# Scalar bias on the copies out of PSUM, one addition per projection, a third bank for q, and lag products with their sides exchanged

## The chip, the cores and the metric

The kernel runs on one core of one Trainium2 chip. The metric is the device time of one execution in microseconds (us): the median of several runs, and beside it one execution that the hardware profiler recorded. The engines are named as the profile names them: PE (TensorE matmul), PEld (TensorE weight load), DVE (VectorE), ACT (ScalarE), POOL (GpSimd) and SP (SyncE, which issues most DMAs here).

## The reference, cut to what matters

One layer over a sequence of 2048 rows of 1024 channels:

```python
hn = rmsnorm(h, g)
u, g_ssm, q, k, v, g_attn = jnp.split(hn @ w_in, SPLITS, axis=-1)    # 512 columns each
y_ssm = s5_branch(u, ...) * silu(g_ssm)         # 32 groups of 16 channels, 64 complex states each
y_att = stick_breaking_branch(q, k, v, ...) * silu(g_attn)           # 8 heads of 64
h = h + concat([y_ssm, y_att]) @ w_out
h = h + sigmoid(rmsnorm(h, g2) @ w_ple_gate) * (p @ w_ple_proj)

# stick breaking, per head and block of 128 queries
z = q @ k.T * scale                             # q and k RMS-normed per head
log_stay = where(s < t, log_sigmoid(-z), 0)
later = reverse_cumsum(log_stay) - log_stay
weights = where(s < t, exp(log_sigmoid(z) + later), 0)
out = weights @ v
```

## The kernel before, in words

**Stages.** The stream runs in five stages. First the norms, the u projection and the tables of the state-space model (0 to some 135 us). Then eight batches of the state-space model, four groups each, between which the gate projection of that branch is worked off (`gate_unit`) and the first four attention projections are made (to some 331 us). Then 40 attention steps `t` (to some 1130 us), four passes of two heads (`hp`) that start eight steps apart (SKEW = 8), so that two passes run at a time. Then the output projection and the gated layer embedding (to the end).

**A batch of the state-space model.** `ssm_pack` (L307) builds for four groups `bn` (128 states x 4 groups x 16 lags x 16 channels) and `mc`. It transposes `bn` into `mb` through PSUM (L340, L341), and then makes the lag products: for each of 2 halves `s` and 4 groups `k` one fp32 matmul with the 128 columns of `bn` as the stationary side and the 16 columns of the group's C matrix as the moving side (L346), all into one bank, copied to `lags` by ACT (L349), corrected by DVE and sent to `lag_d` by SP (L355). `ssm_batch` (L370) reads it back later as a Toeplitz matrix.

**A projection.** `attn_proj` (L706) makes q, k, the gate and v of one block of 128 rows for two heads: 512 columns. From the fifth block on it runs with the contraction cut into two halves of 64 rows that run side by side in the array, each into its own bank (L733, 48 records of 64x512). ACT copies the first bank to `part` (L740, or L736 with the row scale for the first two blocks), and DVE adds the second bank to it in two instructions: 384 columns into `qn` (q, k, gate) and 128 columns into `vr` (v); both show as L65, the line of the helper `vt`. The banks go to the next projection when both have read them. Attention needs v minus the row before it. So SP copies rows 0 to 126 of `vr` one partition down into `v` (L743), and the last row of the previous block into row 0 (L747, one row of 512 bytes), and POOL subtracts (L749). POOL also makes the power of the norm (L501) and the causal fill (L812).

**A block of attention.** `attn_block` (L788) goes through the keys in chunks of up to 512, from the last. For each head z = q k in three float32r products (L805), a sigmoid of -z by ACT (L809), the causal fill by POOL on the diagonal chunk (L812), a running product by DVE (L814, reading z's bank once more), then PE transposes (L520, `ps_wt`), and ACT writes 1 minus the transposed product to `ws` (L828): function Identity, scale -1, and for the bias a column of ones in SBUF, `e.one`. PE multiplies `ws` by v (L836), two heads side by side in two halves of the array's columns.

**Banks.** PSUM has eight banks. `BANKS` (L44) deals out six of them: three to z, two to the projection and one to the output of a block up to step 31, and from step 32 on two, two and one, the rest to the GLU.

**The order of the work.** The order on every engine is written out before the program is built: `plan` (L1293) collects what each instruction depends on, `duration` (L1260) gives each a modelled length, `list_schedule` (L1419) lists them forward and backward for six turns, and the best by its own clock is kept. It charges 0.2 for each change between three kinds of PE work: full array, halves by rows, halves by columns (L1419, `change=0.2`). The hardware queues are in order, so an instruction that waits holds all that stand behind it on its engine or queue.

## Time and profile before

| what | value |
|---|---|
| median of 3 runs | 1534.51 us (1533.57 to 1535.1) |
| the profiled execution | 1535.16 us |
| its span, first to last instruction | 1533.4 us |
| PE, PEld busy | 1467.1, 1247.9 us |
| DVE, ACT, POOL busy | 1011.0, 835.4, 494.7 us |
| mean granted TensorE clock | 0.987 |

The profiled execution is 1.8 us longer than its span and 0.65 us longer than the median of the runs. In the rows, a group is a line, an engine, an operation, out<-in and a shape with its count; then its busy time and the mean duration of one in ns; then the idle time of the engine just before these instructions and which instruction ended it. A wait row gives who waited for whom, the total, the count and the longest. A timeline row gives start, length, engine, line, operation and count; neighbours of one kind are merged. PE records overlap: a record's length holds its passage through the array, and the distance from start to start is what it costs.

### The profile page before, as it was taken

How to read it: one execution, taken by the hardware profiler on the slowest of the kernel's cores; microseconds unless marked ns; L12 is line 12 of the kernel's file. 1: busy time of each engine (PE TensorE's matmuls, PEld its weight loads, DVE VectorE, ACT ScalarE, POOL GpSimd, SP SyncE). 2: the span in 40 equal slices, each digit the busy share in tenths (PEclk: the TensorE clock that was granted, in tenths of full speed). 3: DMA queues.
4: the chain of work that ended last, by engine and by line, in shares of the span. 5: the costliest groups of instructions: out<-in, count | busy, mean ns of one | idle time of the engine just before them, and what ended most of it. 6: DMA issues, size and time to landing. Idle time of an engine off the chain costs nothing. (4 is left out here: it accounts for less than half of the span.)

```text
span 1533.4 us, 33754 instructions
## 1 busy us (share of the span) xinstructions
PE 1467.1 (96%) x13116; PEld 1247.9 (81%) x13116; DVE 1011.0 (66%) x1861; ACT 835.4 (54%) x1756; POOL 494.7 (32%) x530
## 2 busy tenths in 40 slices
PE   6999999989999999999999998999999999999998
PEld 5899989978888888888888877777776888777776
DVE  8933868856666786668766777456668556754543
ACT  5644545546555776567665667555654435633333
POOL 3251344412221211212112244431145654434433
PEclk8999999989999999999999999999999999999999
DMA  8877645555432442334333467754457645522211
GB/s 291 281 258 214 222 139 177 180 164 185 144 123 96 141 132 95 125 111 133 124 114 106 145 222 228 239 159 98 105 181 227 206 161 185 184 63 96 89 63 62
DMA packets 179072, 240.33 MB, mean 157 GB/s; under 512 B 65648, under 2 KB 120928, under 8 KB 167520
## 3 DMA queue, kind: packets, MB, share of 16 engines
q1 hardware_dynamic: 176528, 229.58, 46.3%
q0 software_dynamic: 2384, 8.59, 2.1%
q8 instruction: 104, 1.70, 0.5%
q14 instruction: 56, 0.46, 0.1%
HBM read 169.03 MB, written 64.90 MB: 153 GB/s over the span
## 5 line engine op out<-in xcount | busy, mean ns | idle before, releaser
L814 DVE TENSOR_TENSOR_SCAN px<-px,ps_z 128x512 f32<-128x512 f32 (+3 forms) x320 | 341.3, 1086 | 97.0 <-ACT px L809 62.8
L733 PE MATMUL ps_q<-w_w,xt 64*128 64x512 f32 x2880 | 397.5, 401 | 5.7 <-DVE vr L65 5.3
L733 PEld LDWEIGHTS ps_q<-w_w,xt 64*128 64x128 f32 x2880 | 288.7, 187 | 46.3 <-PE ps_z L805 5.5
L828 ACT ACTIVATE ws<-ps_wt,one 128x512 f32<-128x512 f32 (+3 forms) x320 | 189.0, 626 | 86.5 <-PE ps_wt L520 85.2
L809 ACT ACTIVATE px<-ps_z 128x512 f32<-128x512 f32 (+3 forms) x320 | 159.3, 534 | 57.7 <-PE ps_z L805 56.7
L805 PE MATMUL ps_z<-k,q 64*128 64x512 f32 (+3 forms) x960 | 140.3, 379 | 8.2 <-DVE px L814 6.8
L836 PE MATMUL ps_o<-ws,v 128*64 128x128 f32 x2176 | 137.2, 278 | 2.9 <-ACT ws L828 2.9
L836 PEld LDWEIGHTS ps_o<-ws,v 128*64 128x64 f32 x2176 | 118.6, 138 | 19.6 <-issue 12.6
L520 PEld LDWEIGHTS ps_wt<-ident,px 64*128 64x128 f32 x2176 | 98.2, 139 | 32.8 <-ACT ws L828 15.7
L501 POOL TENSOR_TENSOR rs_qk<-rs_qk,mhalf 128x4 f32<-128x4 f32 x64 | 67.5, 1055 | 144.9 <-DVE rs_qk L72 144.6
L520 PE MATMUL ps_wt<-ident,px 64*128 64x64 f32 x2176 | 105.1, 225 | 9.3 <-ACT ws L828 8.4
L805 PEld LDWEIGHTS ps_z<-k,q 64*128 64x128 f32 x960 | 91.3, 187 | 25.3 <-DVE px L814 9.6
L812 POOL TENSOR_SCALAR_AFFINE_SELECT px<-px 128x128 f32<-128x128 f32 x128 | 40.5, 324 | 211.8 <-ACT px L809 196.7
L749 POOL TENSOR_TENSOR v<-vr,v 128x128 f32<-128x128 f32 x64 | 31.2, 488 | 195.6 <-DMA v<-vr 195.6
L535 PE MATMUL ps_u<-xt,w_w 128*128 128x256 f32 x256 | 75.2, 296 | 8.1 <-ACT w_w L485 6.9
L1008 POOL TENSOR_TENSOR sg<-sg,h 128x512 f32<-128x512 f32 x32 | 44.8, 1411 | 112.7 <-DVE sg L65 112.7
L65 DVE TENSOR_TENSOR yr<-sx,yr 128x512 fp32r<-128x512 f32 x64 | 56.3, 900 | 34.1 <-ACT yr L507 33.1
L537 PE MATMUL ps_u<-xt,w_w 128*128 128x256 f32 x256 | 74.6, 298 | 2.5 <-DVE w_w L76 2.5
L65 DVE TENSOR_TENSOR qn<-ps_q,part 128x384 f32<-128x384 f32 x54 | 29.5, 547 | 71.3 <-ACT part L740 68.7
L536 PE MATMUL ps_u<-xt,w_w 128*128 128x256 f32 x256 | 75.1, 295 | 0.5 <-DVE xt L65 0.5
L507 ACT ACTIVATE yr<-sx 128x512 fp32r<-128x512 f32 x64 | 39.3, 628 | 54.5 <-PE ps_h L703 19.7
L535 PEld LDWEIGHTS ps_u<-xt,w_w 128*128 128x128 f32 x256 | 51.8, 202 | 8.7 <-ACT w_w L485 7.1
(416 smaller groups left out, 3490.6 us busy)
## 6 DMA issues: line engine op xcount, KB each, us to landing
xt<-hn SPq DMA_DIRECT2D x60, 1024.0 KB
hn<-xt SPq DMA_DIRECT2D x16, 1024.0 KB
h<-h SPq DMA_DIRECT2D x64, 256.0 KB
wst<-in_w_in_dram SPq DMA_DIRECT2D x48, 256.0 KB
xg<-hn SPq DMA_DIRECT2D x12, 1024.0 KB
out_dram<-sg SPq DMA_DIRECT2D x32, 256.0 KB
x<-in_x_dram SPq DMA_DIRECT2D x14, 512.0 KB
h<-in_x_dram SPq DMA_DIRECT2D x28, 256.0 KB
```

Source lines behind the costliest of these rows:

```text
L65: nc.vector.tensor_tensor(out, a, b, op=op)
L501: nc.gpsimd.tensor_tensor(r, r, e.mhalf[:, :n], op=ALU.pow)
L520: e.nc.tensor.transpose(ps[h][:, 64 * k:64 * k + 64], v[r], e.ident[r, r])
L535: mm(out, wh, xh, start=first, stop=False)
L536: mm(out, wh, xl, start=False, stop=False)
L537: mm(out, wl, xh, start=False, stop=last)
L733: nc.tensor.matmul(o, xt[r, a, c], A.w[c][r, b], start=c + s == 0, stop=c == NC8 - 1 and s == 2)
L805: nc.tensor.matmul(z[:, :n], q[half[h], a], A.k[ch][half[h], b, :n], start=s == 0, stop=s == 2)
L809: nc.scalar.activation(px[:, :n], z[:, :n], AF.Sigmoid, scale=-(HD ** -0.5))
L814: nc.vector.tensor_tensor_scan(rv, rv, z[:, :n][:, ::-1], initial=1.0 if carry[h] is None else carry[h], op0=ALU.mult, op1=ALU.bypass)
L828: nc.scalar.activation(dst, ps, AF.Identity, bias=e.one, scale=-1.0)
L836: nc.tensor.matmul(po[half[h], :P], A.v[sb][:, h], w[:, h, b], start=sb == i, stop=sb == 0)
```

## The change

It does four things.

1. ACT's copy of the transposed products (L828) becomes function Copy with the number 1.0 as bias, in place of Identity with the column `e.one`; the column and its memset go.
2. `qn` becomes 512 columns wide and holds v too. One DVE addition (or one scaled addition for the first two blocks) writes all of it; for blocks 0 to 3 one ACT copy. `vr` is now a view of `qn`. The last row of a block is sent on to row 0 of the next block's v by the same projection, so the v tile of block i+1 is taken one projection earlier; for block 4, whose place doesn't exist yet, the row rests in a small tile `vl` and is copied on by one more DMA. The row DMA still follows the 127-row DMA in SP's queue.
3. In the attention steps 0 to 5 z has two banks and the projection three; from step 6 on all is as before. The names of the two banks become one name that goes round two or three tags.
4. The lag products: C and its turned form now lie in one tile, so that 32 consecutive columns can be taken from every group on. They are the stationary side, `bn` (256 columns for both halves) is the moving side, and the four groups write four strips of 32 partitions of one bank. ACT copies this to `lt` (a tile shared with `part`), PE transposes it in two pieces into another bank, and ACT copies every first 16 of 32 columns to `lags`. The modelled length of such a matmul is cut to a quarter in `duration`.

```diff
--- before.py
+++ after.py
@@ -41,7 +41,7 @@
 XB, XTB, GTB, QSB, PXB, WSB, SWB, ROTB, STA, STB, STC, ALT, ALT0, ALT1, SSM_STEPS, SSM_DEPTH, PREP0, PXX, WSX, XTX, XT0 = 4, 2, 5, 5, 8, 5, 2, 2, 3, 2, 3, "o", 0, 30, 10, 2, 0, 0, 0, 0, 13
 WE = 6
 AHEAD = 4
-BANKS = (("z0", "z1", "tr"), ("acc","ssm"), ("o",)), (("z0", "z1"), ("acc","tr"), ("o",))
+BANKS = (("z0", "z1", "tr"), ("acc", "ssm"), ("o",)), (("z0", "z1"), ("acc", "tr"), ("o",)), (("z0", "z1"), ("acc", "ssm", "tr"), ("o",))
 WSV = lambda ch: 0
 KV_SLOT = {(0, 0): 0, (0, 1): 1, (0, 2): 2, (1, 0): 3, (0, 3): 4, (1, 1): 5, (1, 2): 6, (2, 0): 7,
            (1, 3): 0, (2, 1): 1, (2, 2): 2, (3, 0): 4, (3, 1): 3, (2, 3): 5, (3, 2): 0, (3, 3): 1}
@@ -199,8 +199,8 @@
 
     bst = sm.tile([P, G, GH], F32, tag="bst", name="bst")
     bsw = sm.tile([P, G, GH], F32, tag="bsw", name="bsw")
-    R.cts = kt("cts", [G, GH])
-    R.ct2 = kt("ct2", [G, GH])
+    R.ct = kt("cts", [2, G, GH])
+    R.cts, R.ct2 = R.ct[:, 0], R.ct[:, 1]
     for d, name in ((bst, "b"), (bsw, "b_turned"), (R.cts, "c"), (R.ct2, "c_turned")):
         dma(d, e.small(name).rearrange("p (g h) -> p g h", g=G))
     vs(nc, R.cts, R.cts, sgn, ALU.mult)
@@ -340,13 +340,19 @@
             nc.tensor.transpose(ps[:, k * P:(k + 1) * P], bnf[:, 4 * q + k], e.ident)
         nc.scalar.activation(mbf[:, 4 * q:4 * q + 4].rearrange("p g m -> p (g m)"), ps, AF.Copy)
     ps = e.bank("ps_pack", "w0", "w1")
+    flat = R.ct.rearrange("p k g h -> p (k g h)")
+    with e.abreast():
+        for k in range(GB):
+            o = (b * GB + k) * GH
+            nc.tensor.matmul(ps[2 * GH * k:2 * GH * (k + 1), :HS * P], flat[:, o:o + 2 * GH], bnf[:, HS * k:HS * (k + 1)].rearrange("p s m -> p (s m)"), start=True, stop=True)
+    lt = e.spare.tile([P, 512], F32, tag="part", name="lt", bufs=1)[:, :HS * P]
+    nc.scalar.activation(lt, ps[:, :HS * P], AF.Copy)
+    ps = e.bank("ps_pack", "w0", "w1")
     for s in range(HS):
-        for k in range(GB):
-            o = (s * GB + k) * GH
-            nc.tensor.matmul(ps[:, o:o + GH], bnf[:, HS * k + s], R.cts[:, b * GB + k, :], start=True, stop=True)
+        nc.tensor.transpose(ps[:, s * P:(s + 1) * P], lt[:, s * P:(s + 1) * P], e.ident)
     lags = sm.tile([P, HS + 1, GB, GH], F32, tag="lags", name="lags", bufs=2)
     nc.vector.memset(lags[:, HS], 0.0)
-    nc.scalar.activation(lags[:, :HS], ps[:, :HS * GB * GH].rearrange("p (s g h) -> p s g h", s=HS, h=GH), AF.Copy)
+    nc.scalar.activation(lags[:, :HS], ps[:, :HS * P].rearrange("p (s g v h) -> p s g v h", s=HS, v=2, h=GH)[:, :, :, 0], AF.Copy)
     q3 = slice(96, P)
     sh3 = [P - 96, GB, GH]
     dg = sm.tile([P, GB, GH], F32, tag="dg", name="dg")
@@ -709,22 +715,28 @@
     if xt is None:
         xt = e.buf("xt", [P, 2, NC8, P], XTB, XTX, F32R)
         e.xdma(xt.rearrange("p s c t -> p (s c t)").bitcast(F32), e.hn_d[i])
-    both = pool.tile([P, 3 * HPP, HD], F32, tag="qn", name="qn", bufs=2)
-    vb = A.v[i] = e.kv_tile(A.hp, i, "v", [P, HPP, HD])
-    vr = pool.tile([P, P], F32, tag=f"vr{A.hp % 2}", name="vr", bufs=2)
-    flat, vf, vb = both.rearrange("p h d -> p (h d)"), vr, vb.rearrange("p h d -> p (h d)")
+    both = pool.tile([P, 4 * HPP, HD], F32, tag="qn", name="qn", bufs=2)
+    if i == 0:
+        A.v[i] = e.kv_tile(A.hp, i, "v", [P, HPP, HD])
+        nc.gpsimd.memset(A.v[i][:1], 0.0)
+    if i + 1 < NT and i + 1 not in A.v:
+        A.v[i + 1] = e.kv_tile(A.hp, i + 1, "v", [P, HPP, HD]) if xt is None or i + 1 < AHEAD else pool.tile([P, HPP, HD], F32, tag="vl", name="vl", bufs=1)
+    if A.v[i].tensor.name.startswith("vl"):
+        row = A.v[i]
+        A.v[i] = e.kv_tile(A.hp, i, "v", [P, HPP, HD])
+        nc.sync.dma_start(A.v[i][:1], row[:1])
+    flat, vb = both.rearrange("p h d -> p (h d)"), A.v[i].rearrange("p h d -> p (h d)")
+    vr = flat[:, 384:]
     if len(e.q_banks) == 1:
         pq = e.bank("ps_qk", *e.q_banks)
         for c in range(NC8):
             mm3x(e, pq, (xt[:, 0, c], xt[:, 1, c]), (A.w[c][:, 0], A.w[c][:, 1]), c == 0, c == NC8 - 1)
         if i < 2:
-            nc.scalar.activation(flat, pq[:, :384], AF.Copy, scale=e.rs[i])
-            vs(nc, vf, pq[:, 384:], e.rs[i], ALU.mult)
+            nc.scalar.activation(flat, pq, AF.Copy, scale=e.rs[i])
         else:
-            nc.scalar.activation(flat, pq[:, :384], AF.Copy)
-            nc.vector.tensor_copy(vf, pq[:, 384:])
+            nc.scalar.activation(flat, pq, AF.Copy)
     else:
-        pq = [e.bank(f"ps_q{h}", tag) for h, tag in enumerate(e.q_banks)]
+        pq = [e.bank("ps_q", *e.q_banks) for h in range(2)]
         for c in range(NC8):
             with e.abreast():
                 for s, (a, b) in enumerate(((0, 0), (0, 1), (1, 0))):
@@ -734,20 +746,15 @@
         part = pool.tile([P, 512], F32, tag="part", name="part", bufs=1)
         if i < 2:
             nc.scalar.activation(part, pq[0], AF.Copy, scale=e.rs[i])
-            stt(nc, flat, pq[1][:, :384], e.rs[i], part[:, :384], ALU.mult, ALU.add)
-            stt(nc, vf, pq[1][:, 384:], e.rs[i], part[:, 384:], ALU.mult, ALU.add)
+            stt(nc, flat, pq[1], e.rs[i], part, ALU.mult, ALU.add)
         else:
             nc.scalar.activation(part, pq[0], AF.Copy)
-            vt(nc, flat, pq[1][:, :384], part[:, :384], ALU.add)
-            vt(nc, vf, pq[1][:, 384:], part[:, 384:], ALU.add)
+            vt(nc, flat, pq[1], part, ALU.add)
     nc.sync.dma_start(vb[1:], vr[:P - 1])
-    if A.last is None:
-        nc.gpsimd.memset(vb[:1], 0.0)
-    else:
-        nc.sync.dma_start(vb[:1], A.last[P - 1:])
-    A.last = vr
+    if i + 1 < NT:
+        nc.sync.dma_start(A.v[i + 1][:1].rearrange("p h d -> p (h d)"), vr[P - 1:])
     nc.gpsimd.tensor_tensor(vb, vr, vb, op=ALU.subtract)
-    raw, gate = both[:, :2 * HPP], flat[:, 256:]
+    raw, gate = both[:, :2 * HPP], flat[:, 256:384]
     gn = pool.tile([P, P], F32, tag="gn", name="gn", bufs=1)
     nc.scalar.activation(gn, gate, AF.Sigmoid)
     vt(nc, gn, gate, gn, ALU.mult)
@@ -825,7 +832,7 @@
             if h and WSV(ch):
                 vs(nc, dst, ps, -1.0, ALU.mult, 1.0, ALU.add)
             else:
-                nc.scalar.activation(dst, ps, AF.Identity, bias=e.one, scale=-1.0)
+                nc.scalar.activation(dst, ps, AF.Copy, bias=1.0, scale=-1.0)
         held.append((ch, nb, w))
         if len(held) == HOLD or ch == 0:
             with e.abreast():
@@ -842,7 +849,7 @@
 
 def attn_pass(e, hp):
     A = Env()
-    A.hp, A.k, A.v, A.q, A.w, A.last = hp, [], {}, {}, [], None
+    A.hp, A.k, A.v, A.q, A.w = hp, [], {}, {}, []
     return A
 
 
@@ -1062,8 +1069,6 @@
     make_identity(nc, e.ident)
     e.mhalf = const("mhalf", [P, 2 * HPP])
     nc.vector.memset(e.mhalf, -0.5)
-    e.one = const("one", [P, 1])
-    nc.vector.memset(e.one, 1.0)
     e.rs = [const(f"rs{i}", [P, 1]) for i in range(2)]
 
     def part(name):
@@ -1135,6 +1140,7 @@
     right, left, far = ExitStack(), ExitStack(), ExitStack()
     kv0 = pool(far, "kv0", side="right")
     ap1 = pool(far, "proj", side="right")
+    e.spare = ap1
     keep = pool(right, "keep", side="right")
     chain = ExitStack()
     sm = pool(chain, "chain", side="right")
@@ -1199,7 +1205,7 @@
     steps = NT + SKEW * (NHP - 1)
     glu_at = steps - 8
     for t in range(steps):
-        e.z_banks, e.q_banks, e.o_banks = BANKS[t >= glu_at]
+        e.z_banks, e.q_banks, e.o_banks = BANKS[2 if t < SKEW - 2 else t >= glu_at]
         for hp in range(NHP):
             if 0 <= t - SKEW * hp < NT:
                 attn_block(e, ap, A[hp], t - SKEW * hp)
@@ -1270,7 +1276,7 @@
         if "float32r" in kind or "bfloat16" in kind:
             return max(cols / 2400.0 + 0.0136, 0.107) / (2 if ins[0][0] <= 64 else 1), 0.11
         half = min(outs[0][0], ins[0][0]) <= 64
-        return (1 if half else 2) * max(cols / 1160.0, 0.056), 0.12
+        return (0.5 if outs[0][0] <= 32 else 1 if half else 2) * max(cols / 1160.0, 0.056), 0.12
     if eng == "Activation":
         return (0.05 if psum else 0.094) + n * 0.00083, 0.065 if psum else 0.03
     if eng == "Pool":
```

## The prediction

> **What bounds the kernel now.** I read the page's busy line first, then busy time by stage, then PE's waits, then the groups and single stretches of the timeline.
>
> ```profile
> span 1533.4 us, 33754 instructions
> PE 1467.1 (96%) x13116; PEld 1247.9 (81%) x13116; DVE 1011.0 (66%) x1861; ACT 835.4 (54%) x1756; POOL 494.7 (32%) x530
> ```
>
> The stages (from:to, length, then PE, PEld, DVE, ACT, POOL busy, each with its count, then the granted clock, DMA share, GB/s):
>
> ```profile
> 135.00:300.00 165.00, 163.74 (x1311) 158.71 (x1310) 124.50 (x222) 81.87 (x190) 67.03 (x41) 1.00 0.62 194
> 300.00:331.00 31.00, 26.89 (x233) 26.20 (x231) 22.57 (x49) 18.14 (x39) 4.84 (x6) 1.00 0.37 114
> 331.00:420.00 89.00, 83.24 (x881) 70.96 (x882) 53.78 (x113) 46.90 (x116) 17.51 (x33) 0.94 0.52 172
> 420.00:1130.00 710.00, 690.72 (x7942) 576.16 (x7938) 483.44 (x820) 444.25 (x968) 175.97 (x265) 1.00 0.44 137
> ```
>
> PE is the bound. From 135 to 300 us it is idle for 1.3 of 165 us, so PE work taken out there shortens the stage. From 300 to 331 us the end of the last state-space batch is waited for (4.1 us idle). In the attention steps PE is idle for 5.8 us up to 420 and 19.3 us after; there ACT or DVE time is worth only what PE waits for. PE's waits, first from 331 to 420 us, then from 420 to 1130 us, and one row of the weight load from 331 to 1130 us (total, count, longest):
>
> ```profile
> PE ps_o L836 <- ACT ws L828: 2.9, 2, 1.6
> PE ps_q L733 <- DVE vr L65: 2.6, 4, 1.0
> ...
> PE ps_wt L520 <- ACT ws L828: 7.9, 9, 1.9
> PE ps_z L805 <- DVE px L814: 5.2, 5, 2.0
> PE ps_q L733 <- DVE vr L65: 2.6, 6, 0.8
> ...
> PEld ps_wt L520 <- ACT ws L828: 15.1, 26, 2.4
> ```
>
> The change touches three of these releasers: ACT's `ws`, DVE's `vr`, and (through POOL) DVE's `px`.
>
> **The lag products.** A stretch of the last batch (start, length, count), then a stretch of attention with column halves:
>
> ```profile
> 294.46 0.60 PE L340 MATMUL ps_pack<-ident,bn 128*128 128x128 f32 x4
> 294.90 0.61 PE L458 MATMUL ps_y<-rot,stC 128*128 128x127 f32 x4
> 295.34 1.86 PE L346 MATMUL ps_pack<-cts,bn 128*128 128x16 f32 x16
> 297.05 0.36 PE L535 MATMUL ps_sg<-xg,w_w 128*128 128x256 f32 x1
> ```
> ```profile
> 709.42 0.65 PE L520 MATMUL ps_wt<-ident,px 64*128 64x64 f32 x16
> 710.00 3.28 PE L836 MATMUL ps_o<-ws,v 128*64 128x128 f32 x56
> 713.21 0.34 PE L520 MATMUL ps_tq<-ident,qn 64*128 64x64 f32 x4
> ```
>
> Removed: 8 matmuls are 16 records and take PE from 295.34 to 297.05, 1.71 us a batch (107 ns a record), although only 16 columns move: the 128 stationary columns set the pace. Added: 4 matmuls of 256 moving columns, two records each. The column halves run side by side in the second stretch: 56 records in 3.28 us less the last one's passage (some 0.27 us), 55 ns a record, hence 109 ns per 128 columns in one half and 219 ns per 256. If four strips run side by side as two halves do, two records cost 0.44 us. Two transposes add 0.22 (four take 294.46 to 294.90). Going into column mode costs about 0.12 more than a record (the last `ps_wt` starts near 709.85, `ps_o` at 710.00), coming out 0.15 (the last `ps_o` starts at 713.01, the next at 713.21): 0.27. New sum 0.93 us, gain 0.78 a batch. No row shows four strips. Bounds over 8 batches: with no change of mode charged, 0.66 us, gain 8.4; with the strips one after another, 8 x 0.219 + 0.49 = 2.24 us, loss 4.2. I take 0.78, nearest to the halves' row, for seven batches, **-5.5 us**, and nothing for the eighth, whose end falls where the batch's own chain is waited for. The added copy on ACT (a 128x256 copy from a bank, 0.38 us) lies beside PE: ACT has 83 us free in that stage. If that cover were gone, 8 x 0.38 = 3 us.
>
> The Trainium skill (TensorEngine Tiling (Array Packing), Instruction Overhead) says that a matmul of one moving column takes as long as one of 60 cycles. By it the 16 old records would cost about 25 ns each, 0.4 us, and the exchange would lose 0.5 us a batch; the row's 107 ns a record speaks against reading it so here, and the time it would give, about that of the rival "no change" below, has no chance beside that rival's. The same skill (TensorE: Matmul & The Clock Gate, Part 3) gives 2.38 times for three column strips; by that efficiency 0.44 us becomes 0.55 and the term -4.7, an estimate from that page.
>
> **The copy with scalar bias.** ACT groups, mean ns behind the busy time:
>
> ```profile
> L828 ACT ACTIVATE ws<-ps_wt,one 128x512 f32<-128x512 f32 x224 | 146.7, 688 | 71.6 <-PE ps_wt L520 70.3 <-PE ps_o L836 0.4
> L341 ACT ACTIVATE stB<-ps_pack 128x512 f32<-128x512 f32 x16 | 9.3, 595 | 2.8 <-PE ps_pack L340 2.8
> ...
> L828 ACT ACTIVATE ws<-ps_wt,one 128x128 f32<-128x128 f32 x32 | 10.9, 370 | 3.0 <-PE ps_wt L520 3.0
> L349 ACT ACTIVATE lags<-ps_pack 128x128 f32<-128x128 f32 x8 | 2.2, 278 | 5.9 <-PE ps_pack L346 5.8
> ```
>
> The same shape from a bank to SBUF takes 93 ns less without a column operand at 512 columns and 92 at 128. 320 instructions (224, 32 of 128, 64 between): 29.7 us of ACT. ACT is not the bound, so the path gains only in PE's waits. `ws` comes in pairs, 0.186 us a pair. PE's 11 waits for it (10.8 us) lose at least 2.0 us and at most all 10.8. The 26 waits of the weight load are nearer to what PE loses, since records hide short gaps: 26 x 0.186 = 4.8. I take the middle of 2.0 and 4.8, **-3.4 us**. Late next is DVE's running product (5.2 us above), which gets its sigmoid sooner but is no faster.
>
> **One addition, and three banks.** DVE groups, then DVE and PE in the first projection of the attention steps, then the tightest place for z:
>
> ```profile
> L65 DVE TENSOR_TENSOR qn<-ps_q,part 128x384 f32<-128x384 f32 x54 | 29.5, 547 | 71.3 <-ACT part L740 68.7 <-PE ps_z L805 2.6
> L65 DVE TENSOR_TENSOR h<-ps_h,h 128x512 f32<-128x512 f32 x40 | 27.3, 687 | 27.3 <-PE ps_h L703 24.1 <-DMA h<-h 3.1
> L65 DVE TENSOR_TENSOR vr<-ps_q,part 128x128 f32<-128x128 f32 x54 | 15.0, 278 | 0.0
> ```
> ```profile
> 346.15 0.56 DVE L65 TENSOR_TENSOR qn<-ps_q,part 128x384 f32<-128x384 f32 x1 [4.52 <-ACT part L740]
> 346.76 0.75 DVE L76 SCALAR_TENSOR_TENSOR w_w<-wst,gmix,w_w 128x512 fp32r<-128x512 f32 x1
> 347.43 0.28 DVE L65 TENSOR_TENSOR vr<-ps_q,part 128x128 f32<-128x128 f32 x1
> ...
> 362.30 2.45 DVE L814 TENSOR_TENSOR_SCAN px<-px,ps_z 128x512 f32<-128x512 f32 x2 [1.25 <-ACT px L809]
> ...
> 364.67 0.53 DVE L65 TENSOR_TENSOR qn<-ps_q,part 128x384 f32<-128x384 f32 x1
> ```
> ```profile
> 347.87 2.98 PE L733 MATMUL ps_q<-w_w,xt 64*128 64x512 f32 x23 [1.02 <-DVE vr L65]
> ...
> 364.22 0.62 PE L805 MATMUL ps_z<-k,q 64*128 64x256 f32 x6
> ```
>
> 547 + 278 = 825 ns become some 687 (the 512-column addition with one side in a bank): 54 x 0.138 = 7.4 us of DVE. On the path it matters that the bank is free at the end of the first addition, not behind a stranger: here a weight split stands between the two, PE waits 1.02 us, and with one addition the bank would be free at 346.84 instead of 347.71. Of the six waits after 420 us (2.6 us) at least 6 x 0.138 = 0.8 goes and at most all; I take half, **-1.3 us**. The four waits before 420 go with the third bank: 2.6 us. It is taken from z. Where z is tightest, the running products of one chunk end at 364.75 and the next z starts at 364.22: with two banks its second head waits some 0.5 us. Bounds for the banks: -2.6 and, if all eight chunks of those steps lost that, +1.4; I take -2.6 + 0.5 = **-2.1 us**.
>
> **The row sent ahead.** SP's row DMA, whom it ends waits for, and one case on SP and POOL:
>
> ```profile
> L747 SPq DMA_DIRECT2D v<-vr x60: 567/1940/7590, 210.6 to 1081.5; - x60
> ...
>   POOL v L749: 177.4, 57
> ```
> ```profile
> 725.88 7.59 SPq L747 DMA_DIRECT2D v<-vr x1
> ```
> ```profile
> 737.26 0.46 POOL L749 TENSOR_TENSOR v<-vr,v 128x128 f32<-128x128 f32 x1 [9.84 <-DMA v<-vr]
> ```
>
> Issuing one row holds SP's queue for 1.94 us in the median, up to 7.59, and POOL's subtraction waits for it 57 times, 177.4 us, with causal fills and norm powers queued behind it on POOL. The DMA stays, with the same shape and place on SP, so whatever is queued behind it there (loads of `xt`, weights) waits as before; but it is for the next block, so POOL stops waiting for it. The added `vl` copy is one more such issue, 2 us once, beside PE. What PE gets is only its waits for `px`: 0 to -5.2 us. PE barely hangs on POOL, so I take **-0.5**. Against that, `qn` is now held until the DMAs and POOL have read v. Of two buffers each is rewritten two additions later, 18.5 us in the densest place (346.15 to 364.67), and the slowest case above needs until 737.72, some 12 us from its DMA issue. I cost it at nothing; that cover goes if three projections come within 12 us.
>
> **The sum.** -5.5 - 3.4 - 1.3 - 2.1 - 0.5 = -12.8 us. The profiled execution took 1535.16 us, which gives 1522.4; the median lies 0.65 lower, so I predict **1522 us**.
>
> **The rivals.**
> - *Slower: the new written order costs more changes of mode.* All lengths and dependencies on DVE and PE shift, so the list is drawn anew for every engine. Place: the 64 attention blocks; price: one more split of a block's `ps_o` costs 0.27 us. If each block is split once more, 64 x 0.27 = 17.3, and the time is 1522 + 17 = 1539 us. It decides from 47 more splits (12.8 / 0.27). For it: PE holds thousands of records whose order nothing fixes. Against: the list charges such a change.
> - *No change: the four strips run one after another.* The first term is +4.2 instead of -5.5, and 1522 + 9.7 is 1531.7; with half the ACT term hidden, 1533.4. Against: the halves run side by side.
> - *Faster, but less: the ACT and POOL terms are taken over by DVE's running product.* Left are -5.5 and -2.1: 1527 us. For it: DVE's scans take 1.2 us each and are not changed.
> - *More: all waits for `ws` and the additions go, with the best lag case.* -8.4 - 10.8 - 2.6 - 2.6 - 0.5 = -24.9: 1510 us.
>
> **How the numbers follow.** Forecast (1514 to 1525) 0.52; faster but less 0.20; more 0.06; no change 0.08; slower 0.14. Within 0.2% means 1531.4 to 1537.6, about what a measurement of this kernel can tell. So faster is 0.78, the same 0.08, slower 0.14. The range runs from 1513, below the forecast's sum with half of the "more" case, to 1534, the upper end of "no change"; some 0.05 lies below and 0.15 above. The likeliest case alone has 1514 to 1525.
>
> **What would show it.** Right: the lag group with few records of 128x256 in four strips, starting within nanoseconds of each other, and less than 1 us of PE a batch; `ws` at 595 ns and ACT's busy time down by some 27 us (29.7 less 3 for the new copies); the addition near 687 ns; no waits for it before 420 us; POOL's waits for v down by most of 177 us; attention starting some 5 us earlier and ending some 12 us earlier. Wrong: strips 0.2 us apart; PE idle or short pieces of L836 up in the attention steps; `qn` additions waiting for POOL or a DMA; z waiting in the first six steps.

## The result and the profile after

The changed kernel takes 1539.77 us in the median (1534.09 to 1546.4) against 1534.92 for the kernel before, measured beside it: a ratio of 1.0029 with a 95% interval of 1.0017 to 1.0041, so 4.5 us slower (2.6 to 6.3). The forecast was 1522. Below, a ratio is turned into microseconds with 1535.

The profiled execution of the changed kernel took 1534.23 us, 5.5 us under the median of its runs and 0.9 us under the profiled execution of the kernel before (1535.16). So its rows show what became of each part of the change, but not the loss of 4.5 us itself. First the page's busy line of the changed kernel, then the parts of the change in its groups (line, engine, out<-in, shape, count; busy us, mean ns; idle time before and its releasers):

```profile
span 1532.4 us, 33569 instructions
PE 1462.1 (95%) x13068; PEld 1235.0 (81%) x13068; DVE 1005.6 (66%) x1796; ACT 812.0 (53%) x1764; POOL 494.0 (32%) x530
```
```profile
L835 ACT ACTIVATE ws<-ps_wt 128x512 f32<-128x512 f32 x224 | 125.0, 599 | 67.3 <-PE ps_wt L526 66.4
L65 DVE TENSOR_TENSOR qn<-ps_q,part 128x512 f32<-128x512 f32 x54 | 36.7, 679 | 57.0 <-ACT part L751 51.1 <-PE ps_z L812 5.9
...
L835 ACT ACTIVATE ws<-ps_wt 128x128 f32<-128x128 f32 x32 | 7.9, 278 | 6.0 <-PE ps_wt L526 6.0
```

Every instruction costs what was forecast: `ws` 599 ns (595), at 128 columns 278 (278), the addition 679 (687). ACT lost 23.4 us of busy time (27 forecast), PE 5.0. The lag products on PE, in one batch (start, length, count):

```profile
293.12 0.28 PE L543 MATMUL ps_sg<-xg,w_w 128*128 128x256 f32 x1
293.33 0.64 PE L347 MATMUL ps_pack<-bn,cts 128*32 128x256 f32 x8
293.90 0.49 PE L464 MATMUL ps_y<-rot,stC 128*128 128x127 f32 x2
```

The eight records of the four strips take PE from 293.24 (the last `ps_sg` start and one step of 0.12) to 293.90, 0.66 us with the change into strips; forecast were 0.44 and 0.27. So the four strips do run side by side. But the time did not follow. By stage, before and then after (from:to, length, then PE, PEld, DVE, ACT, POOL busy with counts, granted clock, DMA share, GB/s):

```profile
135.00:335.00 200.00, 192.99 (x1559) 186.68 (x1557) 149.52 (x274) 101.97 (x234) 72.43 (x48) 0.99 0.59 184
335.00:1130.00 795.00, 771.60 (x8802) 645.35 (x8800) 534.77 (x927) 489.19 (x1077) 192.91 (x296) 0.99 0.44 140
```
```profile
135.00:335.00 200.00, 187.76 (x1496) 175.69 (x1494) 156.56 (x272) 108.22 (x246) 73.93 (x50) 0.97 0.59 185
335.00:1130.00 795.00, 771.34 (x8774) 644.01 (x8776) 524.00 (x863) 458.70 (x1069) 189.58 (x291) 0.99 0.44 139
```

In the state-space stage PE has 5.2 us less to do and is idle 5.2 us longer, at a lower clock: attention's first `ps_o` starts at 331.2 instead of 332.7 us, 1.5 us earlier where 5 were forecast. In the attention steps PE is as busy as before. The clock differs more over all runs than in these rows: its mean is 0.984 in the 20 runs of the changed kernel and 0.988 to 0.989 in the runs of the kernel before that were made beside the experiments. A difference of 0.0045 in 1535 us is some 7 us, an estimate, and more than the loss. POOL's wait for v, of which most was to go, and a new wait on SP (two views of waits: total, count, longest), and what SP issues there (ns min/median/max):

```profile
POOL v L756 <- DMA v<-qn: 190.5, 60, 6.6
...
SPq L727 <- DMA vl<-qn: 91.5, 42, 3.4
```
```profile
L755 SPq DMA_DIRECT2D vl<-qn x48: 524/2334/7958, 236.9 to 1058.3; - x48
...
L727 SPq DMA_DIRECT2D v<-vl x48: 497/518/626, 322.4 to 1061.1; - x48
```

The row rests in `vl` not for block 4 alone, as I had read the code, but for every block from 4 on: `xt` has been filled a few lines above the condition that asks for `xt is None`. So there are 48 additional DMAs, and SP's queue, which also issues the weight loads, stands 91.5 us for the row to land in `vl`.

One stall of the changed kernel shows what such an order can cost. Rows of SP, ACT and PE, then the clock in steps of 2 us:

```profile
703.44 0.59 SPq L486 DMA_DIRECT2D wst<-in_ssm_w_glu_dram  x1
704.08 0.66 SPq L753 DMA_DIRECT2D v<-qn  x1
704.79 7.96 SPq L755 DMA_DIRECT2D vl<-qn  x1
...
707.88 0.63 ACT L513 ACTIVATE w_w<-wst 128x512 fp32r<-128x512 f32 x1 [4.88 <-DMA wst<-in_ssm_w_glu_dram]
...
709.48 1.12 PE L526 MATMUL ps_wt<-ident,px 64*128 64x64 f32 x16 [4.85 <-ACT ws L835]
```
```profile
704.00:706.00 2.00, 0.64 (x12) 0.40 (x8) 0.01 (x1) 0.00 (x0) 0.33 (x1) 1.00 1.04 297
706.00:708.00 2.00, 0.00 (x0) 0.00 (x0) 0.00 (x0) 0.12 (x1) 0.00 (x0) 0.78 0.71 228
708.00:710.00 2.00, 0.52 (x10) 0.52 (x12) 0.92 (x2) 2.00 (x6) 0.29 (x1) 0.50 0.25 98
710.00:712.00 2.00, 2.00 (x20) 1.72 (x18) 1.97 (x4) 1.20 (x3) 1.03 (x2) 0.50 0.24 86
712.00:714.00 2.00, 2.00 (x12) 1.53 (x12) 0.43 (x1) 0.00 (x0) 0.27 (x1) 0.51 0.08 22
714.00:716.00 2.00, 2.00 (x38) 1.84 (x36) 1.00 (x1) 1.45 (x4) 0.01 (x1) 1.00 0.24 50
```

ACT's queue stands at the weight split whose load is late, the copy `ws` is queued behind it, PE waits 4.85 us. The granted clock is at half from 707.12 to 713.95 us, and the work done under it, from 709.48 us on, loses some 2.2 us more. The Trainium skill (TensorE: Matmul & The Clock Gate, Part 1) says that an idle window of some 3.4 us halves the clock and that a busy one brings it back. The trace agrees with the length of the window: here the half clock lasts 6.83 us, and all such pieces after 344 us, in all the traces, last 3.41 us or twice that. It doesn't show that a wait has to last that long: in the same trace a PE wait of 2.72 us at 966 us is followed by 3.41 us of half clock. In the kernel before, PE's longest wait from 335 to 1130 us is 1.99 us. This stall isn't the copies' doing: without them (below) PE's longest wait for `ws` is still 4.4 us.

### The profile page after: what moved, and what is told of

It reads as the page before. It is cut to its first block, busy times and chain, and to the rows that moved or that the text cites. A ratio compares the mean times of both kernels' runs of the same rounds, so it can differ in the third digit from the quotient of the medians.

```text
span 1532.4 us, 33569 instructions
## 1 busy us (share of the span) xinstructions
PE 1462.1 (95%) x13068; PEld 1235.0 (81%) x13068; DVE 1005.6 (66%) x1796; ACT 812.0 (53%) x1764; POOL 494.0 (32%) x530
## 4 chain that ended last, share of the span: by engine, by line
PE 76%; DVE 8%; issue 5%; DMA 4%; ACT 3%; POOL 2%; SPq 1%; POOLq 0%; DVEq 0%; ACTq 0%
PE ps_q L745 20%; PE ps_o L843 6%; PE ps_z L812 6%; PE ps_wt L526 4%; PE ps_g L707 3%; PE ps_g L709 3%; PE ps_h L707 3%; PE ps_g L708 3%; PE ps_h L709 3%; PE ps_h L708 3%; PE ps_sg L541 1%; PE ps_u L542 1%; PE ps_sg L542 1%; PE ps_u L543 1%; PE ps_u L541 1%
## 5 line engine op out<-in xcount | busy, mean ns | idle before, releaser
L835 ACT ACTIVATE ws<-ps_wt 128x512 f32<-128x512 f32 (+3 forms) x320 | 158.6, 535 | 85.3 <-PE ps_wt L526 84.5
L812 PEld LDWEIGHTS ps_z<-k,q 64*128 64x128 f32 x960 | 92.3, 189 | 29.4 <-DVE px L821 10.4
L756 POOL TENSOR_TENSOR v<-qn,v 128x128 f32<-128x128 f32 x64 | 30.1, 470 | 203.4 <-DMA v<-qn 190.5
L65 DVE TENSOR_TENSOR yr<-sx,yr 128x512 fp32r<-128x512 f32 x64 | 52.6, 843 | 33.4 <-ACT yr L513 32.4
L65 DVE TENSOR_TENSOR qn<-ps_q,part 128x512 f32<-128x512 f32 x54 | 36.7, 679 | 57.0 <-ACT part L751 51.1
L541 PE MATMUL ps_sg<-xg,w_w 128*128 128x256 f32 x192 | 56.6, 295 | 2.3 <-DVE sg L65 2.2
```

Source lines behind the costliest of these rows:

```text
L541: mm(out, wh, xh, start=first, stop=False)
L812: nc.tensor.matmul(z[:, :n], q[half[h], a], A.k[ch][half[h], b, :n], start=s == 0, stop=s == 2)
L835: nc.scalar.activation(dst, ps, AF.Copy, bias=1.0, scale=-1.0)
```

## The experiments

Two theories stood from the start: that a part of the change costs more than its work (a new wait, a full queue), or that the written order, drawn anew by the planner for every kernel, decides. The first runs take the parts one by one, each with the order that the planner writes for it.

**The scalar bias alone.** Here the order of the instructions stays that of before on every engine.

```diff
-nc.scalar.activation(dst, ps, AF.Identity, bias=e.one, scale=-1.0)
+nc.scalar.activation(dst, ps, AF.Copy, bias=1.0, scale=-1.0)
```

> The kernel before with the scalar bias alone; the column of ones is still made, so that the written order of every engine stays as before. My theory (each term of the sum is real, something else eats it): ws at 595 ns, ACT's busy time down by some 30 us, 2 to 5 us faster than before. Rival (PE's waits for ACT are taken over by others, or ACT's time was never on the path): ACT down by 30 us and the time within 1 us of before.

Measured: 1533.22 us, ratio 0.9977 (0.9963 to 0.9992), -3.5 us (1.2 to 5.7 faster). The term was -3.4. PE's waits for `ws` fell by only 1.2 us (11.3 to 10.1).

**The lag products alone** (the hunks of `ssm_chain` and `ssm_pack`, and the strips' length in `duration`).

> The kernel before with the lag products exchanged alone. My theory (PE work taken out shortens the stage): some 5 us faster, the first attention block some 5 us earlier. Rival (the stage of the state-space batches is bound by DVE and the batches' chain, not by PE): PE busy 5 us less, the first attention block no more than 2 us earlier, time within 2 us of before. Second rival (the longer lag path makes PE idle and its clock drop): 3 us slower or more.

Measured: 1536.86 us, ratio 0.9999 (0.9984 to 1.0014). PE is busy for 188.2 instead of 193.0 us from 135 to 335 us, and idle for 11.8 instead of 7.0: the whole gain became idle time.

**The projection alone** (the hunk of `attn_proj` without the banks).

> The kernel before with v in qn, one addition and the row sent ahead alone. Theory that the 48 additional row copies through vl and SP's queue eat the gain: 5 us slower or more, with SP waiting some 90 us for vl's rows. Rival (these copies lie beside PE): 1 to 3 us faster, since PE waits less for the additions.

Measured: 1546.74 us, ratio 1.0058 (1.0039 to 1.0078), 9 us slower. Most of it is there before the attention steps begin: the first `ps_o` starts at 343.1 instead of 332.7 us. The copies out of `vl` start only at 322 us, so they can't have made that part of the loss.

**The banks alone** (`BANKS` and the two lines that use it).

> The kernel before with three banks for q and two for z in the steps 0 to 5 alone. My theory: PE no longer waits for the addition before 420 us, 2 us faster. Rival (z with two banks gives it back, or another written order costs more): within 1 us of before or slower.

Measured: 1530.22 us, ratio 0.9953 (0.9935 to 0.997), -7.2 us, more than three times the term.

**The change without the 48 copies**: the row goes straight to its place as soon as the places exist.

```diff
-... if xt is None or i + 1 < AHEAD else pool.tile([P, HPP, HD], F32, tag="vl", name="vl", bufs=1)
+... if given is None or i + 1 < AHEAD else pool.tile([P, HPP, HD], F32, tag="vl", name="vl", bufs=1)   # given = xt as passed in
```

> The changed kernel, but the last row goes straight into the next block's v for every block from the fifth on, without the resting place vl and its 48 additional copies. Theory that these copies in SP's queue delay weight loads: SP's 91 us of waits for vl's row gone, the longest wait of PE for ws back from 4.8 to some 2 us, 4 to 9 us faster than the changed kernel. Rival (the loss of the projection part lies in the written order of the state-space batches): no more than 3 us faster than the changed kernel.

Measured: 1536.17 us, ratio 1.0011 (0.9996 to 1.0026). By the two ratios that is 2.8 us under the change (0.1 over to 5.7 under), less than the forecast 4 to 9 and not clear of noise. PE's longest wait for `ws` was to fall to some 2 us and is still 4.4. So in this order the copies are perhaps half of the loss, and the late weight loads aren't theirs alone.

**The change without the projection part.**

> The changed kernel with the projection part undone (v in its own tile, two additions, rows as before); scalar bias, lag products and banks as changed. Theory that the projection part carries the whole loss and that the other terms add up (bias alone -3.5, lag alone 0, banks alone -7): 1525 us, 10 us faster than before. Rival (the parts don't add, each written order is its own draw): within 5 us of before.

Measured: 1534.6 us, ratio 1.0001 (0.9989 to 1.0013). Bias, lag and banks, -3.5, 0 and -7 alone, give nothing together. Terms measured apart don't add.

**Bias and banks.**

> The kernel before with the scalar bias and the banks alone; the written order of every engine is that of the run with the banks alone. Theory (the bias saves what it saved by itself, since ACT's time is in the same waits): 1527 us, 2 to 4 us faster than the banks alone and 8 to 10 faster than before. Rival (the banks took the same waits away): within 1 us of the banks alone.

Measured: 1529.68 us, ratio 0.9965 (0.9949 to 0.9981): with the banks the bias adds nothing that can be measured.

**No change but another order.** The planner's charge for a change of PE's kind of work goes from 0.2 to 0.25 in the kernel before; in a second run its bonus for an instruction that stays with the same kind of PE work goes from 4.0 to 3.5; in a third the first setting is used with the whole change.

```diff
-def list_schedule(ops, pre, soft, length, mode, rank, near=4.0, change=0.2):
+def list_schedule(ops, pre, soft, length, mode, rank, near=4.0, change=0.25):
```

> A control: the kernel before, not one instruction changed, but the list charges 0.25 in place of 0.2 for a change of PE mode, so that the order on every engine is written anew. Theory that the written order is a draw that weighs as much as the terms of the change: the time moves by 3 us or more in either direction. Rival (the order matters little, the parts' differences are their own): within 1.5 us of before.

> A second control: the kernel before, not one instruction changed, with the list's allowance for staying in a PE mode at 3.5 in place of 4.0. Theory that each written order is a draw: 3 us or more from before in either direction, and PE's idle time plus lost clock in the attention steps moves by as much. Rival: within 1.5 us of before, the first control was an exception.

> The changed kernel with the list's charge for a change of PE mode at 0.25, as in the first control. Theory that the loss of the change is one of its written order and not of its parts: against the control with the same charge (1547.5 us) it is 5 us faster or more, or it lies 4 us or more from the changed kernel (1539.8). Rival (the parts themselves cost): 3 to 6 us slower than that control, and within 3 us of the changed kernel's distance to before.

Measured: 1547.47 us, ratio 1.0088 (1.0072 to 1.0104); 1538.54 us, ratio 1.0038 (1.0015 to 1.0061); and with the change 1542.38 us, ratio 1.0047 (1.0025 to 1.0069). The same instructions in another order are 13.5 us (11.1 to 16.0) or 5.8 us (2.3 to 9.4) slower, more than any term of the sum, and under the first of these settings the change makes the kernel some 6 us faster (by the ratios). The order decides even the sign. It isn't by changes of PE's mode: counted row by row from 335 to 1135 us there are 182 stretches of one kind of work before, 189 after, 186 in the slowest of these. Both new orders of the kernel before are slower than its own; whether its own had once been picked among several by its time isn't on record.

What a worse order costs can be read for the slowest of these. Its profiled execution took 1550.42 us, 15.3 us more than that of before. Its attention steps:

```profile
335.00:1130.00 795.00, 764.58 (x8674) 639.59 (x8675) 524.16 (x916) 482.00 (x1061) 190.39 (x292) 0.98 0.44 138
```

PE is idle 7.0 us longer than before, in waits of up to 3.5 us, and in this window the granted clock is at half for 31.6 us where it was for 10.8. Half of the additional 20.8 us is at most 10.4 us lost, so idle time and half clock together are at most 17.4 us and can hold the 15.3. So a worse order shows itself as longer PE waits with half clock behind them; why this order has them isn't traced.

**VectorE lightened, without and with the lag exchange.** Two multiplications are left out, those of the gate with its sigmoid and of the last product of the GELU, so the output lacks these factors.

```diff
         nc.scalar.activation(sg, o, AF.Sigmoid)
-        vt(nc, sg, o, sg, ALU.mult)
...
-        vt(nc, fl(sq), ps, fl(sq), ALU.mult)
```

> The kernel before without two of DVE's products in the state-space batches: the gate is not multiplied by its sigmoid (32 instructions of 256 columns, 13 us) and y not by its GELU factor (16 of 512 columns, 11 us), so the output lacks these two factors. It is the partner of the next run. Theory that DVE limits these batches together with PE: DVE falls by 24 us there, and the first block of attention starts no more than 3 us earlier, since PE is just as full.

> The same without these two products, with the lag products exchanged. Theory that the exchange gains nothing because DVE (and PE's waits for it) ends the batches: with DVE lighter the 5 us of PE become time, and the first product of weights and v starts some 4 to 6 us earlier than in its partner. Rival (the longer lag path or the written order eats it): it starts within 2 us of its partner, and PE idles 5 us more, as with the lag products alone.

Measured: 1524.05 us, ratio 0.9925 (0.9901 to 0.9948), and with the exchange 1527.75, ratio 0.9961 (0.9947 to 0.9974). The lightened kernel is 11.5 us faster (three runs), but its first `ps_o` starts only 2.5 us earlier (330.2 instead of 332.7); the rest comes later, in attention steps whose order was drawn anew too, so the 11.5 us is no price of VectorE's work in that stage. With VectorE lightened the exchange brings the first `ps_o` 1.7 us forward (330.2 to 328.5), and the kernel still ends 5.5 us later (1.3 to 9.7). A busy VectorE alone doesn't explain why the exchange gives nothing.

**The parts in a held order.** The remaining runs take the planner out of the comparison. The starts that it modelled for one kernel are kept as a table, and each engine's list in another kernel follows them; instructions that the old kernel doesn't have are put behind what they need. The run with the banks alone, below, shows that this holds the order: its DVE, ACT and POOL follow the kernel before instruction for instruction.

```diff
 def arrange(tc, pools, rows):
-    ops, pre, *rest = plan(tc, pools)
-    _, order, _ = best_order(ops, pre, *rest, rows)
+    ops, pre, soft, length, mode = plan(tc, pools)
+    order = by_old_order(ops, pre, soft, length, rows)   # the modelled starts of the kernel before, by name and number
```

The whole change, and the whole change without the copies:

> All four parts, with the 48 copies of a row, but each engine's instructions in the order that the planner wrote for the kernel before: an instruction that both have stands at its old place, the new ones (the transposes of the lags, their copy, the sending of the row) behind what they need. Theory that the new order made the loss: the parts are worth their work here, -3.5 (bias, measured alone), -1 to -5 (lag), -1 to -2 (projection) and +3.6 (the copies, measured) together: 2 to 7 us under before. Rival, that the parts bring waits of their own whatever the order: 0 to 6 us over before, as the kernel of the change (+4.5).

> The same without the 48 copies (the row goes straight to its place from block 4 on). Order theory: 6 to 11 us under before, and 3 to 4 us under the run with the copies. Rival (waits of the parts' own): within 2 us of before, as without the old order (+1.7). If it is within 1 us of the run with the copies, the copies' 3.6 us came from the order as well.

Measured: 1560.36 us, ratio 1.016 (1.0142 to 1.0177), and without the copies 1532.54, ratio 0.9986 (0.9975 to 0.9997). The run with the copies is 24.6 us over the kernel before, far outside both its theory (2 to 7 us under) and its rival (0 to 6 over). The run without them, 2.1 us under, is short of its theory (6 to 11 under) and lies at the edge of its rival (within 2 us). The copies cost some 27 us here (26.7 by the ratios, four runs with them), far above the 2.8 of the planner's order. The two orders put them at different places: the held order puts each copy right behind its row's DMA, ahead of the loads that follow, while the planner puts it later. In the run with copies, SP's waits, then one case on SP, ACT and PE:

```profile
SPq L727 <- DMA vl<-qn: 156.1, 47, 3.7
```
```profile
357.67 3.53 SPq L755 DMA_DIRECT2D vl<-qn  x1
364.49 0.50 SPq L727 DMA_DIRECT2D v<-vl  x1
365.08 0.53 SPq L847 DMA_DIRECT2D ya<-yat  x1
365.67 0.42 SPq L486 DMA_DIRECT2D wst<-in_w_in_dram  x1
...
368.47 0.72 ACT L491 ACTIVATE w_w<-wst,gmix 128x512 fp32r<-128x512 f32 x1 [5.13 <-DMA wst<-in_w_in_dram]
...
369.40 1.11 PE L526 MATMUL ps_wt<-ident,px 64*128 64x64 f32 x16 [5.29 <-ACT ws L835]
```

The row's issue ends at 361.20; the copy waits for its landing until 364.49; the weight load queued behind it leaves at 365.67; ACT waits for that load and PE for ACT, 5.29 us. In the kernel before the same load left at 359.87:

```profile
359.87 0.38 SPq L480 DMA_DIRECT2D wst<-in_w_in_dram  x1
```

From 335 to 1130 us PE is busy for 757.97 us with the copies and for 775.48 without. Against the kernel before (771.60) the run with copies has 13.6 us more of idle PE, and half the clock for 36.2 us instead of 10.8; half of these 25.4 us is 12.7. The two together are 26.3 us, and the profiled execution is 26.6 us longer (1561.72). So this loss is accounted for: PE waits, and the lowered clock behind them.

The lag products and the projection (with the row sent straight), each alone in the old order:

> The lag products exchanged, nothing else, in the old order. Order theory: the 5 us of TensorE work come out, at least in part: 2 to 5.5 us under before. Rival (VectorE and the chain of a batch set the pace of the state-space stage): within 1.5 us of before, and TensorE idle in 135 to 335 us up by about what its busy time lost, as it was in the planner's own order (0.0, idle +4.8).

> The projection part alone (one addition, the row sent ahead and straight to its place), in the old order. Order theory: the loss of 9 us that it had alone was the order's (and 3 to 4 us of it the copies'): here 0 to 3 us under before. Rival (the wide addition or the row sent ahead cost by themselves): 3 to 6 us over before.

Measured: lag 1534.79 us, ratio 0.9998 (0.9986 to 1.0009); projection 1529.91, ratio 0.9964 (0.9951 to 0.9978). The lag run's state-space stage and its wait for the added copy:

```profile
135.00:335.00 200.00, 189.95 (x1515) 177.06 (x1513) 150.46 (x274) 104.67 (x243) 72.06 (x48) 0.99 0.60 185
```
```profile
PE ps_pack L352 <- ACT lt L349: 2.1, 5, 1.1
```

The exchange gives nothing in the old order either: the first `ps_o` starts at 332.8 us (before: 332.7), at the clock of before (0.99). PE is busy 3.0 us less in this window and so idle 3.0 us longer, and 2.1 of these are one new wait, that of the transposes for ACT's `lt`. So the order isn't needed to explain its nothing. The projection is the opposite: 9 us slower in the planner's order with the copies, 5.5 us faster (3.4 to 7.5) in the held one without them. Copies and order changed together between these two; the 2.8 us above is what the copies make in the order of the whole change.

The banks alone in the old order:

> The third bank for q alone, in the old order: every engine's instructions are those of before in the same sequence, only the bank that a q product writes is another. If the gain of the banks (-5 to -7 in the planner's own order, 0.9953) is that of the rotation itself: 3 to 7 us under before here too, and TensorE's waits for the additions gone. If it was the order drawn for it: 0 to 1.5 us under before. (The projection part in the old order has just measured -5, where its own order had +9.)

Measured: 1537.16 us, ratio 1.0011 (0.9999 to 1.0023). The attention steps in two stretches: before, with the banks' own order, and with the old one:

```profile
335.00:390.00 55.00, 51.96 (x540) 44.99 (x540) 32.54 (x67) 29.03 (x70) 11.46 (x21) 0.93 0.53 174
390.00:1130.00 740.00, 719.64 (x8266) 600.36 (x8262) 502.23 (x860) 460.16 (x1008) 181.45 (x275) 1.00 0.44 138
```
```profile
335.00:390.00 55.00, 55.00 (x620) 45.39 (x618) 37.25 (x78) 30.75 (x74) 13.31 (x24) 1.00 0.55 184
390.00:1130.00 740.00, 718.86 (x8252) 600.64 (x8250) 503.32 (x857) 462.28 (x1010) 182.30 (x275) 1.00 0.44 138
```
```profile
335.00:390.00 55.00, 51.23 (x538) 42.87 (x538) 33.26 (x68) 29.33 (x69) 10.94 (x19) 0.92 0.54 178
390.00:1130.00 740.00, 719.29 (x8226) 601.49 (x8222) 498.72 (x856) 457.91 (x1003) 179.61 (x275) 1.00 0.44 137
```

The whole gain of the banks' own order arises before 390 us: there PE gets through 80 more matmuls than before, without an idle moment and at the full clock from 335.4 us on, which before came back at 342.4; after 390 us the three are alike. The idle time that is gone is 3.0 us and half of the 7.0 us of half clock is 3.5, together most of the 7.2. All the places at which the two orders differ lie there too (40 of DVE's 1861 instructions, 37 of ACT's 1756). In that stretch the new order uses the third bank, as PE and DVE show:

```profile
341.95 3.38 PE L733 MATMUL ps_q<-w_w,xt 64*128 64x512 f32 x28
...
342.93 0.28 DVE L65 TENSOR_TENSOR vr<-ps_q,part 128x128 f32<-128x128 f32 x1
```

PE starts the next projection at 341.95 us while DVE still has to read a bank of the last one, until 343.21; with two banks it would have had to wait for that. In the old order the bank is there and gives nothing: before 420 us PE's waits for the additions fall from 2.6 to 1.0 us, but its waits for `px`, none before, are 2.4 us. So the -7 us need an order made for the bank. Whether that order would give them without the bank was not run.

At last three parts (bias, banks, and the projection with the row sent straight; no lag exchange) in the order written for the banks:

> Scalar bias, banks and projection (the row sent straight to its place, no copies), without the lag exchange, in the order that the planner wrote for the banks alone (0.9953 by itself). If gains measured in a held order add: -7 (that order), -5 (projection), 0 to -3 (bias): 1522 to 1526 us, under both kernels and every run so far. If they are one and the same slack that each of them takes: 1528 to 1531, as the banks alone. Above 1533, if the row sent ahead suits the order of before but not this one.

Measured: 1521.8 us (1519.13 to 1526.55), ratio 0.9904 (0.9883 to 0.9925), 14.7 us faster than the kernel before (11.5 to 18.0) and the fastest of the kernels that leave nothing out. Its attention steps:

```profile
335.00:1130.00 795.00, 773.77 (x8882) 643.05 (x8880) 535.87 (x876) 469.02 (x1087) 194.45 (x299) 0.99 0.46 143
```
```profile
PE ps_z L807 <- DVE px L816: 8.0, 6, 3.5
PE ps_wt L520 <- ACT ws L830: 7.3, 9, 1.6
PE ps_q L740 <- DVE qn L65: 1.3, 4, 0.4
```

The sum of -7.2 (banks in their order), -5.5 (projection) and -3.5 (bias), -16.2, lies within the interval. So does the sum without the bias, -12.7, and beside the banks the bias had added nothing that could be measured; the run can't tell the two apart. PE's longest wait for `ws` is 1.6 us, and the waits for the addition are down from 5.3 us in 10 to 1.3 in 4.

## Why the prediction was wrong, step by step

**The step that failed for the sign: the written order, costed at nothing but changes of mode.** The text said that the list is drawn anew for every engine and then charged only 0.27 us a split, with a chance of 0.14. Another order moves the kernel before by +13.5 and +5.8 us without changing an instruction, at nearly the same count of mode changes. What the order costs is PE waits and the half clock behind them: in the run with the copies held they make up the loss, and the changed kernel runs at a mean clock of 0.984 where before has 0.988 to 0.989. In the order of before, the whole change without the copies is 2.1 us faster (0.5 to 3.8), in the planner's 1.7 slower (0.6 faster to 4.0 slower). The rival's time, 1539 us, came true by luck: its mechanism, more changes of mode, did not (182 stretches before, 189 after). The rival "faster, but less", 1527 us, had also dropped the term of -1.3 without saying so; without that it would have been 1525.6.

**The step that failed for the size: terms that were to add.** Each part was also measured in the order of before (us against before; the bias keeps that order by itself):

| part, in the order of before | forecast | measured |
|---|---|---|
| scalar bias | -3.4 | -3.5 |
| lag products | -5.5 | -0.3 |
| one addition and the row sent ahead | -1.8 | -5.5 |
| three banks | -2.1 | +1.7 |
| sum of the four | -12.8 | -7.7 |
| the four together, without the copies | | -2.1 |
| the same in the planner's order | | +1.7 |
| with the copies: the change | | +4.5 |

From -12.8 to +4.5 some 5 us are mis-sized terms, 5.5 (1.2 to 9.8) are lost where the four come together although the order is held, 3.8 (0.9 to 6.7) are the planner's order and 2.8, not clear of noise, the copies. Why the parts don't add even in a held order stays open; the two largest errors among the terms follow.

**"The added `vl` copy is one more such issue, 2 us once."** A reading error: 48 copies. They cost perhaps 2.8 us in the planner's order, not clear of noise, and some 27 in the held one. In the held one that isn't by their own issue (0.5 us each) but because SP's in-order queue stands at a copy until the row has landed, with weight loads behind it. That question, who is queued behind the waiting instruction, was asked for the row and not for the copy.

**"PE work taken out there shortens the stage."** It didn't. The price of the strips was right (0.66 us where 0.71 was forecast, the forecast's own sum being 0.93 with transposes), so some 6 us of records left the stage; but in the held order the stage ended at the same time. So a PE busy for 163.74 of 165 us was not what set its length. The added ACT copy, said to lie beside PE, stands between two PE steps: it is 2.1 us of PE's waits, and some 3.6 us counted from start to start, since the last records of a batch still count as busy while they pass. Where the rest of the 6 us went the rows don't say; that other work had filled the gaps of a batch's chain before is likely, but not shown. The term of -5.5 is 0 (2.1 faster to 1.4 slower).

**The scalar bias, -3.4:** right in size, -3.5 alone (1.2 to 5.7), with ACT at 600 ns where 595 was forecast. The middle, taken from PE's waits for `ws`, is in part luck: these fell by 1.2 us only, while those for the weight load fell by 3.3 (15.1 to 11.8). It does not add to every order: beside the banks it gave nothing that could be measured.

**One addition and the row sent ahead, -1.3 and -0.5:** too small. Together, without copies and in the held order, -5.5. The reason given for the row was wrong: POOL did not stop waiting, 173.6 us in that run against 195.6 before, because the row's DMA had only been the last of two: before, it ended 57 of POOL's 61 waits, and with the row out of the way the DMA of the 127 rows, queued ahead of it, ends 58. PE's waits for the addition went from 5.3 to 1.3 us, 4.0 us of the 5.5, where I took half of the late six.

**Three banks, -2.1:** nothing in the order of before (0.2 faster to 3.5 slower), -7.2 in an order made for them. In the held order PE's waits for the additions went only from 5.3 us in 10 to 4.2 in 9, and new waits took their place.

**Open:** why one order has more long waits than another, and why the parts don't add where the order is held. One chain is traced (a late weight load, ACT, PE, then the lowered clock), in the changed kernel and in the run with the copies held. The banks' order without the third bank, three parts in the order of before, and the projection with the copies in that order, without the other parts, weren't tried.

## What to carry to other kernels

Where a planner writes the order, a small edit's measured time is the edit plus a new draw: hold the order to the old one and measure the edit, then draw orders for the kernel that results. A held order isn't neutral either: the copies cost some 27 us at the place that it gave them, the banks gave nothing in it, and the parts didn't add. Ask of every wait added to an in-order queue what stands behind it, above all on the queue that issues the loads. And a PE that reads 99% busy in a stage is no proof that its work sets the length of that stage: see whether a chain through other engines has to end there.

## What the runs showed of the hardware

A wait of PE of 4.85 us (at 704 us in the changed kernel) was followed by work at half the granted clock that lost some 2.2 us more. After 344 us the half clock comes in pieces of 3.41 us or twice that in all the traces. All 10 PE waits of 3.45 us or more were followed by it, and 19 of the 27 waits of 2.0 to 3.0 us, so no sharp threshold shows. SP's issue of one 128-element row was held for 2.3 us in the median and for 7.96 us in the worst case; that one ran from 704.79 to 712.75 us while the DMA engines' share fell from 1.04 to 0.24, so full DMA engines don't explain its length, and the cause is open. A copy that waits in SP's queue for another DMA holds the loads behind it: 156.1 us of waits in 47 cases, some 27 us of the kernel. And the runs of one kernel spread with the clock: those of the changed kernel from 1534 to 1546 us, at a mean granted clock from 0.990 down to 0.979.
